# Sixteen of 22 input chunks of a down projection by seven products of sums of blocks

## The chip, the cores and the metric

The kernel runs on one core of a Trainium2 chip. Its time is device microseconds for one execution. The engines are TensorE (PE: matmuls; PEld: its weight loads), VectorE (DVE), ScalarE (ACT), GpSimd (POOL) and SyncE (SP, which here only starts DMAs). Each takes its own queue of instructions, and they wait for each other by semaphores. SBUF is the memory on the chip, PSUM the banks into which matmuls write (eight banks of 128 partitions x 512 float32).

## The reference

Two residual layers over 512 tokens of width 1024: the first mixes tokens by gated linear attention, the second by softmax attention. After each comes the same feed-forward block, in float32:

```python
def conv_ffn(h, w_up, w_conv, b_conv, w_down):
    u = h @ w_up                      # 1024 -> 2 x 2816
    u = depthwise conv of width 3 over tokens(u, w_conv) + b_conv
    val, gate = jnp.split(u, 2, axis=-1)
    return (jax.nn.silu(gate) * val) @ w_down      # 2816 -> 1024

x = x + conv_ffn(rmsnorm(x, norm_ffn[i]), ...)
```

2816 = 22 chunks of 128, and 1024 = 8 chunks of 128. The change is in the last product, `@ w_down`.

## The kernel before, in words

Data lie features by tokens: a tile has 128 features on the partitions and 512 tokens in the free dimension. The residual is held in eight tiles `x[0..7]`. A float32 product is made of three matmuls of a rounded type (float32r): each operand is split into a high part and a low part, and `mm3` (L266 to L268) adds high x high, high x low and low x high into one PSUM bank. Each matmul has a 128 x 128 weight block as its stationary operand and 512 tokens moving.

**Weights** come through the class `Weights`. A list `todo` holds them in the order of use. `make` loads 1 MB (16 blocks of 128 x 128) on SyncE's queue into one of two `raw` buffers (L118), and splits each half of it: the high part `wh` by ScalarE (L143), the low part `wl` by VectorE as raw minus high (L144), 128 x 1024 each, in three buffers of each. Some weights of the attention are split in another way: ScalarE writes the high part (L123) and the negative high part (L124), and an adding DMA started by GpSimd puts the raw weights on top (`flush`, L133). `half` returns the half that is wanted and makes one more ahead.

**The feed-forward block** `ffn` has two stages. In the first, for each m of 22, two `feature_tile`s (24 matmuls each) fill a bank with value and gate of chunk m (`up`). VectorE takes them out (`u`, L603), ScalarE and VectorE do the convolution (L605 to L607), ScalarE the silu (L609), VectorE the product (L610), and a split makes the high and low part (`gu`, L612 and L613) of chunk m. All 22 are kept in SBUF. In the second stage, for each output chunk c of 8, 22 `mm3` (one for each k) add up in one bank (`dn`); VectorE adds the bank to `x[c]` (L625), and the next stage's norm starts on that chunk (`nxt.chunk(c)`: scaled high part, low part, square), or, in the last layer, SyncE stores it.

The tile framework orders each engine's queue by priorities when the kernel is built, and puts in the semaphore waits. Banks come by name: `acc` three, `s` two, `pt` two, `po` one. `big` gives a 128 x 1024 tile from 22 buffers named `g`.

Of the kernel before, what the change touches and what calls it, by code (L numbers as in the profile page):

```python
# [8 lines left out]
F32 = mybir.dt.float32  # L9
# [26 lines left out]

O_STEPS = (22, 23, 25, 27, 29, 31, 32, 33, 34, 35, 36, 37)


# [7 lines left out]
def hybrid_encoder_kernel(  # L47
# [55 lines left out]
    class Weights:  # L103
# [6 lines left out]
        def add(self, src):  # L110
            for i in range(src.shape[0]):
                self.todo += [(src, i, 0), (src, i, 1)]

        def make(self, key):
            src, i, h = key
            if h == 0 and (id(src), i) not in self.raw:
                t = sp.tile([P, 4 * S], F32, tag="raw", bufs=2, name=nm("raw"))
                sync.dma_start(t, src[i])  # L118
                self.raw[id(src), i] = t
            r = self.raw[id(src), i][:, h * 2 * S : (h + 1) * 2 * S]  # L120
            hi, lo = pair("wh", 3, F32R, "wh"), pair("wl", 3, F32R, "wl")
            if any(src is a and i < n for a, n in self.by_dma):
                act.activation(hi, r, AF.Copy)  # L123
                act.activation(lo, r, AF.Copy, scale=-1.0)  # L124
# [20 lines left out]

        def half(self, src, n):
            key = (id(src), n // 2, n % 2)
            self.flush()
            while key not in self.made:
                self.make(self.todo.pop(0))  # L150
            if self.todo:
                self.make(self.todo.pop(0))
            return self.made.pop(key)

    W = Weights()
    up = [w_up[i] for i in range(2)]
    down = [w_down[i] for i in range(2)]
    for a in (w_vg, w_kq, w_gout, up[0], down[0]):
        W.add(a)
    qk_order = [w_akq[i : i + 1] for i in range(w_akq.shape[0])]  # L160
    for a in qk_order[:2] + [w_av] + qk_order[2:] + [w_aout, up[1], down[1]]:
        W.add(a)
    W.by_dma += [(a, 1) for a in qk_order + [w_av]] + [(w_aout, 2)]

# [114 lines left out]
    def feature_tile(*a):  # L279
        for _ in feature_steps(*a):  # L280
            pass
# [61 lines left out]
    def gla(norm, nxt):  # L343
# [40 lines left out]
        sync.dma_start(rraw, w_r)  # L384
        rw = pair("wh", 3, F32R, "rw")
        rv = rraw.rearrange("p (k o c) -> p k o c", k=KC, o=1)
# [199 lines left out]
    def ffn(layer, norm, cw, nxt):  # L586
        hl = []
        for m in range(FC):
            res, pss = [], []
            for t in range(2):  # L590
                ps = bank("s" if t else "acc", "up")
                feature_tile(*W.half(up[layer], 2 * m + t), norm.hl, ps)
# [17 lines left out]
            dve.tensor_tensor(res[0], res[0], res[1], ALU.mult)  # L610
            t = big(F32R, "gu")
            act.activation(t[:, :S], res[0], AF.Copy)  # L612
            dve.tensor_tensor(t[:, S:], res[0], t[:, :S].bitcast(F32), ALU.subtract)  # L613
            hl.append((t[:, :S], t[:, S:]))
        cur = None
        for c in range(KC):
            ps = bank("acc", "dn")
            for k in range(FC):
                u = c * FC + k
                if u % 8 == 0:  # L620
                    cur = W.half(down[layer], u // 8)
                sl = slice((u % 8) * P, (u % 8 + 1) * P)
                mm3(ps, cur[0][:, sl], cur[1][:, sl], *hl[k], k == 0, k == FC - 1)
            if nxt is not None or c < KC - 1:
                dve.tensor_tensor(x[c], x[c], ps, ALU.add)  # L625
                if nxt is not None:
                    nxt.chunk(c)
                else:
                    sync.dma_start(out[c * P : (c + 1) * P, :], x[c])
            else:  # L630
                for sl, queue in ((slice(0, S // 2), sync), (slice(S // 2, S), act)):
                    dve.tensor_tensor(x[c][:, sl], x[c][:, sl], ps[:, sl], ALU.add)
                    queue.dma_start(out[c * P : (c + 1) * P, sl], x[c][:, sl])


# [219 lines left out]
def _layout(inputs):  # L855
# [55 lines left out]
    dn = i["ffn_w_down"].reshape(2, FC, P, KC, P)  # L911
    dn = dn.transpose(0, 3, 1, 2, 4).reshape(2, KC * FC // 16, 16, P, P)
    a["w_down"] = con(dn.transpose(0, 1, 3, 2, 4).reshape(2, -1, P, 4 * S))
    return a
# [19 lines left out]
```

## Time and profile before

| what | value |
|---|---|
| median of 3 runs | 1133.23 us (1132.77 to 1133.43) |
| the profiled execution | 1133.16 us, its span 1131.4 us |
| TensorE busy | 1125.7 us (99%), 5260 matmuls |
| VectorE, ScalarE, GpSimd busy | 690.1, 482.1, 76.0 us |
| the two down projections | 528 matmuls each, the first matmuls at 469.5 and 1008.0 us of the span |
| granted TensorE clock | 1.0 |

A row of the profile names line, engine, operation, output <- inputs with shapes and a count; behind the bar are busy time in us, the mean ns of one, and the idle time of the engine just before such instructions, with what ended it. The chain names the work that ended last, followed back from the end. A timeline row has start and duration in us. The table by stretches has for each stretch its length, then each engine's busy us with the instruction count, the granted clock, the DMA share and GB/s.

### The profile page before, as it was taken

The numbers are of one execution on the slowest core, as the hardware profiler recorded it, in microseconds if no ns is written. First come the engines' busy times: TensorE is split into PE (matmuls) and PEld (weight loads), VectorE is DVE, ScalarE is ACT, GpSimd is POOL, SyncE is SP. The second block draws the span as 40 slices with busy tenths as digits, with TensorE's granted clock in tenths as the row PEclk, the third lists the DMA queues.
The fourth block names the chain that finished last, engine by engine and source line by source line (L and its number), as shares of the span: only waits on it lengthen the run. The fifth ranks groups of instructions, "written<-read, shape, count | busy, mean of one in ns | idle before, by whom it ended". The sixth has DMA issues, their size and how long they took to land.

```text
span 1131.4 us, 12991 instructions
## 1 busy us (share of the span) xinstructions
PE 1125.7 (99%) x5260; PEld 939.2 (83%) x5260; DVE 690.1 (61%) x996; ACT 482.1 (43%) x690; POOL 76.0 (7%) x66
## 2 busy tenths in 40 slices
PE   9999999999999999999999999999999999999998
PEld 7888888888888888888888888888888888888887
DVE  6787563677777777633325589766777777762221
ACT  5564232444444444422234667644444444442210
POOL 0104110000000000000004433000000000000000
PEclk9999999999999999999999999999999999999999
DMA  6422211232322323223247633223232232323320
GB/s 231 149 75 78 84 63 38 75 112 75 112 97 90 112 75 112 100 86 112 77 152 181 149 76 75 56 75 112 75 112 85 101 112 75 112 84 121 130 93 19
DMA packets 19980, 111.66 MB, mean 99 GB/s; under 512 B 2384, under 2 KB 3024, under 8 KB 8400
## 3 DMA queue, kind: packets, MB, share of 16 engines
q1 hardware_dynamic: 17328, 102.29, 25.9%
q0 software_dynamic: 2304, 8.39, 3.9%
q8 instruction: 41, 0.67, 0.2%
q10 hardware_dynamic: 288, 0.15, 0.0%
q14 instruction: 19, 0.16, 0.0%
HBM read 100.34 MB, written 2.10 MB: 91 GB/s over the span
## 4 chain that ended last, share of the span: by engine, by line
PE 99%; DVE 0%; DMA 0%; ACT 0%; issue 0%; SPq 0%; DVEq 0%; ACTq 0%
PE up L266 14%; PE up L267 14%; PE up L268 14%; PE vg L297 8%; PE op L323 8%; PE dn L266 7%; PE dn L268 7%; PE dn L267 7%; PE o L548 2%; PE pt L802 1%; PE av L297 1%; PE kv L524 1%; PE A L266 1%; PE A L268 1%; PE A L267 1%; PE B L266 1%
## 5 line engine op out<-in xcount | busy, mean ns | idle before, releaser
L143 ACT ACTIVATE wh<-raw 128x1024 fp32r<-128x1024 f32 x164 | 173.3, 1056 | 351.4 <-PE up L267 132.8
L144 DVE TENSOR_TENSOR wl<-raw,wh 128x1024 fp32r<-128x1024 f32 x164 | 203.7, 1242 | 144.8 <-ACT wh L143 144.6
L266 PE MATMUL up<-xhl,wh 128*128 128x512 f32 x704 | 274.3, 390 | 0.0
L268 PE MATMUL up<-xhl,wl 128*128 128x512 f32 x704 | 273.9, 389 | 0.0
L267 PE MATMUL up<-xhl,wh 128*128 128x512 f32 x704 | 273.9, 389 | 0.0
L268 PEld LDWEIGHTS up<-xhl,wl 128*128 128x128 f32 x704 | 132.2, 188 | 27.6
L266 PEld LDWEIGHTS up<-xhl,wh 128*128 128x128 f32 x704 | 132.2, 188 | 27.4
L267 PEld LDWEIGHTS up<-xhl,wh 128*128 128x128 f32 x704 | 132.2, 188 | 27.1
L266 PE MATMUL dn<-gu,wh 128*128 128x512 f32 x352 | 136.9, 389 | 0.0
L267 PE MATMUL dn<-gu,wh 128*128 128x512 f32 x352 | 136.9, 389 | 0.0
L268 PE MATMUL dn<-gu,wl 128*128 128x512 f32 x352 | 136.9, 389 | 0.0
L603 DVE TENSOR_TENSOR u<-up,R 128x512 f32<-128x512 f32 x88 | 60.3, 687 | 52.7 <-PE up L268 52.7
L297 PE MATMUL vg<-wh,xhl 128*128 128x512 f32 x256 | 79.7, 390 | 0.6 <-DVE halfneg L184 0.6
L605 ACT ACTIVATE y<-u,cw 128x512 f32<-128x512 f32 x88 | 71.2, 811 | 20.4 <-DVE u L603 20.4
L268 PEld LDWEIGHTS dn<-gu,wl 128*128 128x128 f32 x352 | 66.1, 188 | 13.8
L267 PEld LDWEIGHTS dn<-gu,wh 128*128 128x128 f32 x352 | 66.1, 188 | 13.7
L266 PEld LDWEIGHTS dn<-gu,wh 128*128 128x128 f32 x352 | 66.1, 188 | 13.6
L323 PE MATMUL op<-oT,wh 128*128 128x512 f32 x256 | 70.9, 395 | 0.0
L607 DVE SCALAR_TENSOR_TENSOR y<-u,cw,y 128x511 f32<-128x511 f32 x88 | 65.9, 751 | 2.9
L606 DVE SCALAR_TENSOR_TENSOR y<-u,cw,y 128x511 f32<-128x511 f32 x88 | 65.6, 746 | 0.6 <-ACT y L605 0.6
L609 ACT ACTIVATE y<-y 128x512 f32<-128x512 f32 x44 | 27.9, 634 | 87.8 <-DVE y L607 87.8
L297 PEld LDWEIGHTS vg<-wh,xhl 128*128 128x128 f32 x256 | 48.0, 188 | 10.6 <-ACT sq L240 0.7
(186 smaller groups left out, 1432.1 us busy)
## 6 DMA issues: line engine op xcount, KB each, us to landing
raw<-in_w_up_dram SPq DMA_DIRECT2D x44, 1024.0 KB, 4.8
raw<-in_w_down_dram SPq DMA_DIRECT2D x22, 1024.0 KB, 4.8
wl<-raw POOLq DMA_DIRECT2D x16, 512.0 KB, 4.7
raw<-in_w_vg_dram SPq DMA_DIRECT2D x6, 1024.0 KB, 4.7
raw<-in_w_akq_dram SPq DMA_DIRECT2D x5, 1024.0 KB, 5.2
raw<-in_w_kq_dram SPq DMA_DIRECT2D x4, 1024.0 KB, 4.8
raw<-in_w_gout_dram SPq DMA_DIRECT2D x4, 1024.0 KB, 4.8
raw<-in_w_aout_dram SPq DMA_DIRECT2D x4, 1024.0 KB, 4.9
```

The lines of the kernel that those rows point to most:

```text
L143: act.activation(hi[:, sl], r[:, sl], AF.Copy)
L144: dve.tensor_tensor(lo[:, sl], r[:, sl], hi[:, sl].bitcast(F32), ALU.subtract)
L266: mm(ps, wh, mh, start=start, stop=False)
L267: mm(ps, wh, ml, start=False, stop=False)
L268: mm(ps, wl, mh, start=False, stop=stop)
L297: mm(ps[j][:, :width], hl[k][i == 2][:, j * P : (j + 1) * P], (wl if i == 1 else wh)[:, sl], start=k == 0 and i == 0, stop=k == KC - 1 and ...
L323: mm(pss[ng][n], wt[:, sl], mv, start=k == 0 and i == 0, stop=k == KC - 1 and i == 2)
L603: dve.tensor_tensor(u, ps, norm.R, ALU.mult)
L605: act.activation(y, u, AF.Identity, scale=w(1), bias=w(3))
L606: dve.scalar_tensor_tensor(y[:, 1:], u[:, : S - 1], w(0), y[:, 1:], ALU.mult, ALU.add)
L607: dve.scalar_tensor_tensor(y[:, : S - 1], u[:, 1:], w(2), y[:, : S - 1], ALU.mult, ALU.add)
L609: act.activation(res[1], res[1], AF.Silu)
```

## The change: products of sums of blocks

The 2 x 2 blocks are: two input chunks (k = 2p, 2p+1), two output chunks (c = 2n, 2n+1), and two halves of the tokens (256 each). Before, such a block of the product takes eight half-width products. Now it takes seven, of sums and differences of blocks (Winograd's form of Strassen's scheme): four sums of weight blocks, four of token blocks, and the results are put together from running sums.

- Chunks 0 to 15 make eight pairs. `prepare` makes a pair's token-side sums (two on GpSimd, two on VectorE) and splits them: three `gu` tiles and half a tile for each pair.
- Pairs 0 to 3 are used in part 0, after the up chunk m = 9, and pairs 4 to 7 in part 1, after m = 17 (`DOWN_AFTER`). The pair of m = 8 and 9 is prepared inside part 0, after the second pair of outputs.
- A part has four output pairs n. For each, seven products of 4 chunk pairs x 3 matmuls, 256 tokens wide. Product 1 goes to bank r1; ScalarE copies r1 into r2, onto which product 6 adds; ScalarE copies r2 into the first half of r3, product 5 adds to r2, ScalarE copies r2 into the second half of r3, product 4 adds to r3's first half, product 3 to r2. Product 7 has its own bank r4, product 2 adds to r1. VectorE adds r1, r2, r3 and r4 into x[2n] and x[2n+1]. Product 1 of pair n+1 is issued ahead of product 3 of pair n.
- A 1 MB load of down weights now holds the 16 blocks of one n in one part. `summed` makes four pieces of it: piece 0 and 1 with VectorE sums and the split by ScalarE and VectorE, piece 2 (plain blocks) by ScalarE twice and the adding DMA of GpSimd, piece 3 half as wide. Up to three pieces are made ahead in a part, in four buffers of `wh` and of `wl` (three before). The scratch for GpSimd's DMA descriptors is set to 8192 bytes.
- Chunks 16 to 21 keep the `mm3` of 512 tokens, behind the last up chunk, in the order `PLAIN`: outputs 0 to 3 for k = 16 to 19, then k = 20 and 21 for these, then outputs 4 to 7.
- The host lays out the down weights in the new order.

```diff
+NQ, NPART = 4, 2
+PLAIN = ([(c, k) for c in range(4) for k in range(16, 20)] + [(c, k) for c in range(4) for k in (20, 21)]
+         + [(c, k) for c in range(4, 8) for k in range(16, 22)])
+DOWN_AFTER = {9: 0, 17: 1}
...
-            hi, lo = pair("wh", 3, F32R, "wh"), pair("wl", 3, F32R, "wl")
+            hi, lo = pair("wh", 4, F32R, "wh"), pair("wl", 4, F32R, "wl")
...
+        def summed(self, raw, sums, h):
+            a21, a11, a12, a22 = (raw[:, n * S : (n + 1) * S] for n in range(4))
+            if h == 0:
+                sums["e"] = e = big(F32, "sum")
+                dve.tensor_tensor(e[:, :S], a21, a22, ALU.add)
+                dve.tensor_tensor(a21, a21, a11, ALU.add)
+                r = raw[:, : 2 * S]
+            elif h == 1:
+                e = sums["e"]
+                dve.tensor_tensor(e[:, S:], e[:, :S], a11, ALU.add)
+                r = e
+            elif h == 2:
+                r = raw[:, 2 * S :]
+            else:
+                e = sums["e"]
+                r = tmp("sq", "sum4")
+                dve.tensor_tensor(r, e[:, S:], a12, ALU.add)
+                hi, lo = (sp.tile([P, S], F32R, tag="sq", bufs=3, name=nm(n)) for n in ("wh4", "wl4"))
+                act.activation(hi, r, AF.Copy)
+                dve.tensor_tensor(lo, r, hi.bitcast(F32), ALU.subtract)
+                return hi, lo
+            hi, lo = pair("wh", 4, F32R, "wh"), pair("wl", 4, F32R, "wl")
+            if h == 2:
+                act.activation(hi, r, AF.Copy)
+                act.activation(lo, r, AF.Copy, scale=-1.0)
+                self.pending.append((lo, r))
+            else:
+                act.activation(hi, r, AF.Copy)
+                dve.tensor_tensor(lo, r, hi.bitcast(F32), ALU.subtract)
+            return hi, lo
...
+        def prepare(p, y1, y2):
+            q = tmp("t", "q")
+            b11, b12, b21, b22 = y1[:, :H], y1[:, H:], y2[:, :H], y2[:, H:]
+            pool.tensor_tensor(q[:, :H], b22, b12, ALU.subtract)
+            pool.tensor_tensor(b12, b11, b12, ALU.subtract)
+            t = [big(F32R, "gu") for _ in range(3)]
+            if p % 2 == 0:
+                quads["half"] = big(F32R, "gu")
+            t4 = quads["half"]
+            split(y2, t[1])
+            split(y1, t[0])
+            dve.scalar_tensor_tensor(q[:, H:], b12, -1.0, b22, ALU.mult, ALU.subtract)
+            split(q, t[2])
+            dve.scalar_tensor_tensor(b21, q[:, H:], -1.0, b21, ALU.mult, ALU.subtract)
+            o = (p % 2) * H
+            split(b21, t4, o, H)
...
+        def down_part(part, then):
...
+            def product(n, i, dst, start):
+                h, o = PLACE[i]
+                if (n, h) not in pieces:
+                    pieces[n, h] = W.piece(src, part * NQ + n, h, 3)
+                wh, wl = pieces[n, h]
+                for j in range(NQ):
+                    sl = slice(o + j * P, o + (j + 1) * P)
+                    mh, ml = pairs[j][i]
+                    for a, (w, m) in enumerate(((wh, mh), (wh, ml), (wl, mh))):
+                        mm(dst, w[:, sl], m, start=start and j == 0 and a == 0, stop=j == NQ - 1 and a == 2,
+                           skip_group_check=True)
+                W.flush()
+            def begin(n):
+                r = st[n]
+                r[1] = bank("acc", "r1")
+                product(n, 1, r[1][:, :H], True)
+                r[2] = bank("acc", "r2")
+                act.activation(r[2][:, :H], r[1][:, :H], AF.Copy)
+            begin(0)
+            for n in range(NQ):
+                r, c, d = st[n], x[2 * n], x[2 * n + 1]
+                r1, r2 = r[1][:, :H], r[2][:, :H]
+                product(n, 6, r2, False)
+                r3 = bank("s", "r3")
+                act.activation(r3[:, :H], r2, AF.Copy)
+                r4 = bank("pt", "r4")
+                product(n, 7, r4[:, :H], True)
+                product(n, 2, r1, False)
+                product(n, 5, r2, False)
+                act.activation(r3[:, H:], r2, AF.Copy)
+                dve.tensor_tensor(c[:, :H], c[:, :H], r1, ALU.add)
+                product(n, 4, r3[:, :H], False)
+                if n + 1 < NQ:
+                    begin(n + 1)
+                two = lambda a: a.rearrange("p (o t) -> p o t", t=H)
+                dve.tensor_tensor(two(d), two(d), two(r4[:, :H]).to_broadcast([P, 2, H]), ALU.subtract)
+                dve.tensor_tensor(d, d, r3, ALU.subtract)
+                product(n, 3, r2, False)
+                dve.tensor_tensor(c[:, H:], c[:, H:], r2, ALU.add)
+                if n == 1 and then is not None:
+                    then()
...
+            if m in DOWN_AFTER:
+                down_part(DOWN_AFTER[m], (lambda: prepare(m // 2, last, y)) if m < 2 * NQ * NPART else None)
```

More of the change, by code (lines that the diff above doesn't have):

```diff
@@ L586, in ffn, with act_up @@
     def ffn(layer, norm, cw, nxt):
-        hl = []
-        for m in range(FC):
+        plain = {}
+        quads = {}
+        def act_up(m):
             res, pss = [], []
@@ L610, in ffn @@
             dve.tensor_tensor(res[0], res[0], res[1], ALU.mult)
[L611 to L623, printed above, removed]
+            return res[0]
@@ new lines, in ffn @@
+        PLACE = {1: (0, S), 7: (0, 0), 6: (1, S), 5: (1, 0), 2: (2, 0), 4: (2, S), 3: (3, 0)}
+        def down_part(part, then):
+            src = down[layer]
+            pairs = [quads.pop(part * NQ + i) for i in range(NQ)]
+            st = [{} for _ in range(NQ)]
+            pieces = {}
+            def product(n, i, dst, start):
[39 more added lines that the diff above has]
+                    then()
@@ L633, in ffn @@
                     queue.dma_start(out[c * P : (c + 1) * P, sl], x[c][:, sl])
+        last = None
+        for m in range(FC):
+            y = act_up(m)
+            if m >= 2 * NQ * NPART:
+                t = big(F32R, "gu")
+                split(y, t)
+                plain[m] = (t[:, :S], t[:, S:])
+            elif m % 2 == 0:
+                last = y
+            elif m not in DOWN_AFTER:
+                prepare(m // 2, last, y)
+            if m in DOWN_AFTER:
+                down_part(DOWN_AFTER[m], (lambda: prepare(m // 2, last, y)) if m < 2 * NQ * NPART else None)
+        cur, open_ = None, {}
+        for u, (c, k) in enumerate(PLAIN):
+            if u % 8 == 0:
+                cur = W.half(down[layer], NPART * NQ * 2 + u // 8)
+            sl = slice((u % 8) * P, (u % 8 + 1) * P)
+            if c not in open_:
+                open_[c] = bank("s" if c == 3 else "acc", "dn")
+            mm3(open_[c], cur[0][:, sl], cur[1][:, sl], *plain[k], k == 2 * NQ * NPART, k == FC - 1)
+            if k == FC - 1:
+                end(c, open_[c])
     def attention(norm, nxt):
```

64 lines of the change are left out of this document (50 added, 14 removed).

## The prediction

> **What bounds the kernel now.** I read the page's busy shares first, then the chain that ended last, then the groups of the down projection.
>
> ```profile
> PE 1125.7 (99%) x5260; PEld 939.2 (83%) x5260; DVE 690.1 (61%) x996; ACT 482.1 (43%) x690; POOL 76.0 (7%) x66
> ...
> PE 99%; DVE 0%; DMA 0%; ACT 0%; issue 0%; SPq 0%; DVEq 0%; ACTq 0%
> PE up L266 14%; PE up L267 14%; PE up L268 14%; PE vg L297 8%; PE op L323 8%; PE dn L266 7%; PE dn L268 7%; PE dn L267 7%; PE o L548 2%; PE pt L802 1%; PE av L297 1%; PE kv L524 1%; PE A L266 1%; PE A L268 1%; PE A L267 1%; PE B L266 1%
> ...
> L266 PE MATMUL dn<-gu,wh 128*128 128x512 f32 x352 | 136.9, 389 | 0.0
> L267 PE MATMUL dn<-gu,wh 128*128 128x512 f32 x352 | 136.9, 389 | 0.0
> L268 PE MATMUL dn<-gu,wl 128*128 128x512 f32 x352 | 136.9, 389 | 0.0
> ```
>
> TensorE is the whole chain, and the down projection never waits (idle 0.0). So a matmul taken away is worth its full step, and a wait put into TensorE's queue costs its full length. The 389 ns is the latency of one matmul, not its step: matmuls overlap. The step comes from the table by stretches, and that of a half-width matmul from the only long run of them, the attention's values (av).
>
> ```profile
> core 0: us, PE busy (x) PEld busy (x) DVE busy (x) ACT busy (x) POOL busy (x), PEclk, DMA share, GB/s
> ...
> 600.00:770.00 170.00, 169.74 (x967) 145.06 (x966) 121.59 (x247) 101.92 (x175) 42.45 (x34) 1.00 0.39 101
> ...
> 613.90:625.30 11.40, 11.40 (x96) 11.37 (x95) 8.46 (x11) 6.91 (x10) 4.89 (x4) 1.00 0.53 144
> 250.00:450.00 200.00, 200.00 (x884) 165.62 (x883) 145.05 (x186) 88.63 (x111) 0.00 (x0) 1.00 0.29 100
> ```
>
> ```profile
> 614.09 11.52 PE av L297 x96
> ```
>
> ```profile
> L297 PE MATMUL av<-wh,xhl 128*128 128x256 f32 x64 | 11.7, 283 | 0.0
> ```
>
> Width 512 steps 200.00/884 = 0.226 us. Width 256 steps 11.52/96 = 0.120 us by the chain, not 0.113: halving the width saves 47%, because each matmul carries about 0.013 us that does not shrink. The granted clock is 1.00 in both stretches.
>
> **The saving on TensorE.** Per layer 16 chunks x 8 outputs x 3 matmuls = 384 of width 512 go: 384 x 0.2262 = 86.9 us. In come 2 parts x 4 output pairs x 7 products x 4 chunk pairs x 3 = 672 of width 256: 672 x 0.1200 = 80.6 us. That leaves 6.2 us a layer, 12.4 us in both. One product is 12 matmuls, 1.44 us; an output pair is 7 products, 10.1 us.
>
> [...]
>
> **What hides beside TensorE.** Prices:
>
> ```profile
> 350.06 0.69 DVE L603 TENSOR_TENSOR u<-up,R 128x512 f32<-128x512 f32 x1 [1.31 <-PE up L268]
> ...
> 354.37 0.69 DVE L610 TENSOR_TENSOR y<-y,y 128x512 f32<-128x512 f32 x1 [0.76 <-ACT y L609]
> 355.76 0.69 DVE L613 TENSOR_TENSOR gu<-y,gu 128x512 fp32r<-128x512 f32 x1 [0.70 <-ACT gu L612]
> 356.37 0.68 DVE L603 TENSOR_TENSOR u<-up,R 128x512 f32<-128x512 f32 x1
> 356.97 1.22 DVE L144 TENSOR_TENSOR wl<-raw,wh 128x1024 fp32r<-128x1024 f32 x1
> 358.10 0.75 DVE L606 SCALAR_TENSOR_TENSOR y<-u,cw,y 128x511 f32<-128x511 f32 x1
> 358.88 0.75 DVE L607 SCALAR_TENSOR_TENSOR y<-u,cw,y 128x511 f32<-128x511 f32 x1
> ```
>
> ```profile
> L143 ACT ACTIVATE wh<-raw 128x1024 fp32r<-128x1024 f32 x164 | 173.3, 1056 | 351.4 <-PE up L267 132.8 <-PE dn L267 127.5 <-PE op L323 34.0
> L605 ACT ACTIVATE y<-u,cw 128x512 f32<-128x512 f32 x88 | 71.2, 811 | 20.4 <-DVE u L603 20.4
> L609 ACT ACTIVATE y<-y 128x512 f32<-128x512 f32 x44 | 27.9, 634 | 87.8 <-DVE y L607 87.8
> ...
> L525 ACT ACTIVATE sa<-kv 128x256 f32<-128x256 f32 x8 | 3.1, 384 | 8.3 <-PE kv L524 8.3
> ```
>
> ```profile
> L441 DVE TENSOR_TENSOR ga<-ga,t 128x256 f32<-128x256 f32 x8 | 3.3, 418 | 0.0
> ```
>
> ```profile
> L482 POOL TENSOR_TENSOR end<-ek,fk 128x384 f32<-128x384 f32 x8 | 8.4, 1066 | 4.8 <-DVE ek L478 4.8
> ```
>
> Back to back on VectorE a 512-wide operation takes 0.60 (356.37 to 356.97), a 1024-wide one 1.13, a scalar-tensor-tensor 0.78. In the up projection a pair of chunks adds 0.60 + 0.42 + 2 x 0.42 = 1.9 us of VectorE to 2 x 10.9 us. VectorE was busy 145 of 200 us, so it goes from 73% to 81%; two GpSimd operations of about 1066 x 256/384 = 711 ns a pair lie beside it. TensorE there needs only the weight pieces, which the fourth buffer lets run further ahead: I charge nothing, and if that cover went, 8 pairs x 1.9 x 2 = 30 us bounds it. In a part, an output pair costs VectorE 4 x 0.60 (sums) + 2 x 1.13 + 0.60 (low parts) + 2 x 0.42 + 2 x 0.60 (into x), 7.3 us, and ScalarE 4 x 1.06 + 0.63 + 3 x 0.38 = 6.0 us: both fit 10.1 us, but not by much, so order in the queues decides. The remaining plain stage keeps the 0.226 us step; its last chunk is wanted 17 x 3 x 0.226 = 11.5 us after the last up matmul and is ready 6.4 us after it (350.06 to 356.45): free.
>
> **What the new waits cost.** TensorE now waits for ScalarE's copies between banks, and ScalarE and VectorE take their queues in order. I followed the built order of each engine. Three places:
>
> (a) *Start of a part.* Product 6 adds onto r2, which ScalarE first copies from r1. In ScalarE's queue that copy stands behind the activation for the second half of the last up chunk (m = 9 or 17), and that one waits for VectorE. Count from the end of up's first half for m = 8 (TensorE 0; the part starts at 3 x 5.43 = 16.3). VectorE is late from preparing pair 3: its chain runs 5.0 us to the product y (350.06 to 355.06), then two GpSimd operations, ScalarE copies and five VectorE operations, 8.9 us in all from 5.4 us earlier, so 3.5. Then 21 operations stand before the activation's input: 13 x 0.60 + 6 x 0.78 + 2 x 1.13 = 14.7, so 18.2; activation 0.81 and copy 0.38 give 19.4. TensorE is there at 16.3 + (12 + 5) x 0.12 = 18.3, five matmuls of r4 being put between. Stall 1.1 us; in part 1 the copies of the third weight piece and of the fourth's high part stand in ScalarE's queue in its place, and the same count gives 19.4 against 18.3 again. Bounds: 0 if VectorE is on time, 2.4 with the full durations (0.69, 0.75, 1.22) in place of the steps, 1.3 more. Four parts: 4.4 us.
>
> (b) *r3 before product 4.* Product 5 ends r2, ScalarE copies it into r3, product 4 needs r3. In the built order the high part of the next pair's third weight piece goes first, and its buffer is freed by that same product 5: 0.16 (a result lands 0.283 - 0.120 after the next start) + 1.06 + 0.38 + 0.05 to pass on = 1.65 against the 11 matmuls of the next product 1, 1.32: 0.33, and a restart.
>
> ```profile
> 701.18 0.50 PE L266 MATMUL s<-k,q 128*128 128x512 f32 x1 [0.26 <-ACT p L784]
> 701.51 0.39 PE L267 MATMUL s<-k,q 128*128 128x512 f32 x1
> ```
>
> The restart is 0.33 between starts instead of 0.23, 0.1. So 0.4 a time, three times in part 0; in part 1 the first has no cover, 0.16 + 0.38 + 0.1 = 0.65, then twice 0.4. The fourth pair has three up matmuls as cover in both. Sum 2.65 a layer, 5.3 us. Bounds: 0, if r3's copy were first, and 1.0 each (16 us) if nothing covered.
>
> (c) *The low part by DMA.* The third piece gets its low part as ScalarE's negative copy plus an adding DMA.
>
> ```profile
> 623.13 1.04 ACT L124 ACTIVATE wl<-raw 128x1024 fp32r<-128x1024 f32 x1
> ```
>
> ```profile
> 624.47 0.87 POOL L133 DMA_DIRECT2D wl<-raw  x1 [2.86 <-ACT wl L124]
> ```
>
> ```profile
> wl<-raw POOLq DMA_DIRECT2D x16, 512.0 KB, 4.7
> ```
>
> ```profile
> DMA to landing us min/median/max: 4.5/4.7/9.1
> ```
>
> From product 5's end: 0.16 + 1.06 + 0.38 + 1.05 + 0.3 (624.17 to 624.47) + 4.7 = 7.65. Its first reader comes 62 matmuls later, 7.44, plus the 0.4 of (b): 7.84. So 0.2 us of slack; in part 1's second pair, where VectorE also waits for a load behind this DMA, it is late by about 0.2: 0.4 us in two layers.
>
> Sum: 4.4 + 5.3 + 0.4 = 10.1 lost of 12.4 gained, **2.3 us faster**. The profiled execution was 1133.16 us (span 1131.4, 1.8 around it), 0.07 under the median of 1133.23, so 1130.8.
>
> **The rivals.**
>
> *The waits are hidden.* If VectorE starts each part on time (a) goes, and (b) shrinks to the copies: 1133.2 - 12.4 + 0 to 6 = 1121 to 1127, middle 1124. For it: TensorE lost 0.26 us in the whole attention stage (600 to 770), with VectorE 72% and ScalarE 60% busy.
>
> *The adding DMA decides (slower).* Every pair but a part's first takes its low part from a DMA with 0.2 us to spare; 12 pairs do. A landing of 4.9 us is the point from which it costs; against it, the median is 4.7 and no load need run beside it, since the next load waits for this very DMA. For it: the longest landing was 9.1. At 6.0, 1.1 x 12 = 13 us more: 1144.
>
> *VectorE is later at the start of a part (slower, small).* GpSimd beside VectorE and the full durations make (a) 2.4 to 3.5 instead of 1.1: 5 to 10 us more, 1136 to 1140.
>
> *The step halves.* In a long run 256 might cost 0.2262/2 = 0.113: 672 x 0.007 = 4.7 us a layer, 1121.4. [...] The 96 matmuls of av are long enough that I give it little.
>
> **How the numbers follow.** This kernel's measurement can tell about 0.2%, 2.3 us, from no change. Forecast case (1127 to 1135): 0.42; waits hidden: 0.24; adding DMA: 0.14; VectorE later: 0.18; halved step 0.02. Faster by over 0.2% (under 1130.9): 0.21 + 0.24 + 0.02 = 0.47. Slower (over 1135.5): 0.14 + 0.18, with 0.01 of the forecast's upper tail, 0.33. The same: 0.20. Range 1122 to 1142: it cuts the far end of the hidden case and of the DMA case.
>
> **What would show it.** Steps of r1 to r4 matmuls at 0.120; idle of TensorE in front of r2 of about 1 us released by ScalarE once a part (a), in front of r3 0.3 to 0.6 us three times a part (b), and next to none released by DMA at r1 (c). Without idle at r2 the first rival holds; with idle at r1 after a DMA the second. A step off 0.120 by 0.007 moves the result by 9 us, and idle in the up projection would mean that VectorE's 81% was not free.

## The result, and the profile after

The changed kernel takes 1136.93 us (median of 6 runs, 1136.25 to 1139.34), the kernel before 1133.15 us beside it (6 runs, 1132.77 to 1135.96). The ratio is 1.0032, 95% interval 1.0019 to 1.0045: 3.8 us slower. The profiled execution took 1136.9 us with a span of 1135.2 us, at a granted clock of 1.00.

The page of the kernel after: busy shares, the chain by engine, and the adding DMAs.

```profile
PE 1119.9 (99%) x5836; PEld 957.2 (84%) x5836; DVE 793.1 (70%) x1204; ACT 551.2 (49%) x818; POOL 121.4 (11%) x114
...
PE 86%; DVE 6%; DMA 2%; issue 2%; ACT 2%; POOL 1%; SPq 0%; DVEq 0%; ACTq 0%; POOLq 0%
...
wl<-raw POOLq DMA_DIRECT2D x32, 512.0 KB, 4.6
```

TensorE is still 99% busy, but the chain has changed: before, it was TensorE for 99%, now for 86%. VectorE, ScalarE, GpSimd and DMAs have come into it. A chain that leaves the fullest engine runs through the places where that engine waits. Where they lie is told by the starts of the stages on TensorE. Timeline of the kernel after: the first matmul of feed-forward 0, of the attention, of feed-forward 1, and the last matmul.

```profile
230.47 0.39 PE L332 MATMUL up<-xhl,wh 128*128 128x512 f32 x1
...
591.91 0.39 PE L332 MATMUL A<-xhl,wh 128*128 128x512 f32 x1
...
769.87 0.39 PE L332 MATMUL up<-xhl,wh 128*128 128x512 f32 x1
...
1130.88 0.39 PE L334 MATMUL dn<-gu,wl 128*128 128x512 f32 x1
```

The same four rows of the kernel before.

```profile
228.76 0.39 PE L266 MATMUL up<-xhl,wh 128*128 128x512 f32 x1
...
589.22 0.39 PE L266 MATMUL A<-xhl,wh 128*128 128x512 f32 x1
...
767.17 0.39 PE L266 MATMUL up<-xhl,wh 128*128 128x512 f32 x1
...
1127.40 0.39 PE L268 MATMUL dn<-gu,wl 128*128 128x512 f32 x1
```

| stage on TensorE | before, us | after, us | difference |
|---|---|---|---|
| up to the first up matmul | 228.76 | 230.47 | +1.71 |
| feed-forward 0 | 360.46 | 361.44 | +0.98 |
| attention | 177.95 | 177.96 | 0.0 |
| feed-forward 1 | 360.23 | 361.01 | +0.78 |
| behind the last matmul, to the end of the span | 4.0 | 4.3 | +0.3 |

So each feed-forward block, which was to gain 6.2 us, lost almost 1. And the stage ahead of it, which the diff doesn't seem to touch, lost 1.7.

The granted clock and the step of the new products, in two stretches of the kernel after (columns as before: length, busy us and count of each engine, clock, DMA share, GB/s).

```profile
252.00:340.00 88.00, 88.00 (x389) 72.85 (x389) 70.33 (x102) 43.42 (x58) 7.91 (x9) 1.00 0.24 84
372.00:380.60 8.60, 8.60 (x74) 8.60 (x73) 5.09 (x7) 3.98 (x6) 0.86 (x1) 1.00 0.55 137
```

In the second, TensorE steps through 256-wide products without a wait; from start to start nearly all of them are 0.12 us apart. The first lies in the up projection: TensorE never idles there, with VectorE at 80%. The saving was there, and waits took more than all of it. The waits by line, kernel after (total us, times, longest):

```profile
PE r L730 <- ACT r L739: 5.7, 4, 1.6
...
PE z L483 <- DVE rst L472: 1.3, 1, 1.3
PE r L730 <- ACT r L752: 1.0, 2, 0.5
PE r L730 <- DVE wl L174: 0.9, 2, 0.6
...
PE r L730 <- DMA wl<-raw: 0.2, 1, 0.2
```

This view counts only idle time. What a wait costs is seen in the starts: the part's length, less 336 steps of 0.12 and three up matmuls of 0.226 put into it, leaves 2.49 and 4.85 us lost in parts 0 and 1 of layer 0, 2.69 and 4.43 in layer 1; 14.5 in all. Each wait in it carries another 0.10 us of restart.

**The first copy of a part.** Timeline of the kernel after, start of part 0 on TensorE, VectorE and ScalarE:

```profile
342.00 0.28 PE L730 MATMUL r<-gu,wl 128*128 128x256 f32 x1
...
344.13 0.50 PE L730 MATMUL r<-gu,wh 128*128 128x256 f32 x2 [1.25 <-ACT r L739]
...
342.27 0.69 DVE L672 TENSOR_TENSOR u<-up,R 128x512 f32<-128x512 f32 x1
...
342.99 0.81 ACT L674 ACTIVATE y<-u,cw 128x512 f32<-128x512 f32 x1 [1.27 <-DVE u L672]
343.71 0.36 ACT L739 ACTIVATE r<-r 128x256 f32<-128x256 f32 x1
```

The copy of r1 into r2 (L739) needs none of these up values: r1's last matmul (342.00) was done at 342.3, 1.4 us earlier. It waits because it is queued behind the activation, and that waits for VectorE. In the starts the wait is 1.41 us in part 0 and 1.78 in part 1, and 0.10 more each for the restart.

**The ring behind the adding DMA.** A stretch of the chain of the kernel after, part 1 of layer 0:

```profile
472.43 4.56 DMA wl<-raw
...
477.12 4.99 DMA raw<-in_w_down_dram
...
482.82 1.79 DVE wl L174 x2
484.61 4.93 DMA wl<-raw
...
489.59 3.85 PE r L730 x30
```

The adding DMA reads `raw`, so the next load into that buffer starts only when it has landed (476.98). VectorE's sum for the pair after next waits for that load, and the low parts of the next pair are queued behind this sum. TensorE's first reader of the next adding DMA starts 0.05 us after it has landed. From 472.43 to 489.59 no TensorE work is in the chain. The chain puts that second DMA behind VectorE; the timeline of VectorE and ScalarE has more:

```profile
482.13 0.69 DVE L150 TENSOR_TENSOR sum<-raw 128x512 f32<-128x512 f32 x1 [1.15 <-DMA raw<-in_w_down_dram]
...
482.33 1.05 ACT L169 ACTIVATE wh<-raw 128x1024 fp32r<-128x1024 f32 x1
483.27 1.04 ACT L170 ACTIVATE wl<-raw 128x1024 fp32r<-128x1024 f32 x1
```

The DMA (484.61) follows ScalarE's negative copy, which ended at 484.31; 15 of the 16 adding DMAs of the parts start about 0.3 us behind that copy. So VectorE's wait of 1.15 us makes low parts late, and it is ScalarE's queue that makes this DMA late.

**The stage ahead.** Timeline of the kernel before, around the gate weights (`gst`) of the first mixer:

```profile
32.48 0.21 DVE L379 CAST smask<-gconst 128x128 uint8<-128x128 f32 x1
...
30.22 2.39 POOL L395 TENSOR_TENSOR gst<-graw,gst 32x1024 fp32r<-32x1024 f32 x1
...
28.57 1.04 ACT L394 ACTIVATE gst<-graw 128x1024 fp32r<-128x1024 f32 x1
```

And of the kernel after:

```profile
32.56 2.36 DVE L445 CAST smask<-gconst 128x128 uint8<-128x128 f32 x1
...
32.43 2.40 POOL L461 TENSOR_TENSOR gst<-graw,gst 32x1024 fp32r<-32x1024 f32 x1 [2.22 <-ACT gst L460]
...
30.28 1.06 ACT L190 ACTIVATE wh<-raw 128x1024 fp32r<-128x1024 f32 x1 [6.11 <-DMA raw<-in_w_vg_dram]
31.25 1.04 ACT L460 ACTIVATE gst<-graw 128x1024 fp32r<-128x1024 f32 x1
...
39.37 0.47 PE L483 MATMUL z<-rst,gst 128*128 128x512 f32 x1 [1.31 <-DVE rst L472]
```

With a fourth buffer, ScalarE's split of one more weight half may stand ahead of the gate weights, and it waits until 30.28 for its load. The copy of the gate weights follows it 2.7 us later than before, and GpSimd's subtraction 2.2 us later. That now falls beside VectorE's small cast, which took 0.21 us and now takes 2.36. Everything behind it on VectorE is late, and `z`, which had no wait, waits 1.31 us.

### The profile page after: what moved, and what is told of

Same layout as the page of the kernel before. It is cut to its first block, busy times and chain, and to the rows that moved or that the text cites. A ratio compares the mean times of both kernels' runs of the same rounds, so it can differ in the third digit from the quotient of the medians.

```text
span 1135.2 us, 14636 instructions
## 1 busy us (share of the span) xinstructions
PE 1119.9 (99%) x5836; PEld 957.2 (84%) x5836; DVE 793.1 (70%) x1204; ACT 551.2 (49%) x818; POOL 121.4 (11%) x114
## 4 chain that ended last, share of the span: by engine, by line
PE 86%; DVE 6%; DMA 2%; issue 2%; ACT 2%; POOL 1%; SPq 0%; DVEq 0%; ACTq 0%; POOLq 0%
PE r L730 12%; PE up L333 12%; PE up L332 12%; PE up L334 11%; PE op L389 8%; PE vg L363 7%; PE dn L334 2%; PE dn L333 2%; PE dn L332 2%; PE o L614 2%; DMA wl<-raw 1%; PE pt L968 1%; PE av L363 1%; PE kv L590 1%; DMA raw<-in_w_down_dram 1%
## 5 line engine op out<-in xcount | busy, mean ns | idle before, releaser
L190 ACT ACTIVATE wh<-raw 128x1024 fp32r<-128x1024 f32 x132 | 139.0, 1056 | 212.7 <-PE up L333 114.3
L191 DVE TENSOR_TENSOR wl<-raw,wh 128x1024 fp32r<-128x1024 f32 x132 | 163.8, 1241 | 52.4 <-ACT wh L190 52.4
L730 PE MATMUL r<-gu,wh 128*128 128x256 f32 x896 | 164.5, 285 | 7.1 <-ACT r L739 5.7
L730 PEld LDWEIGHTS r<-gu,wh 128*128 128x128 f32 x896 | 139.1, 191 | 11.8 <-ACT r L739 6.6
L730 PE MATMUL r<-gu,wl 128*128 128x256 f32 x448 | 125.5, 285 | 1.1 <-DVE wl L174 0.9
L730 PEld LDWEIGHTS r<-gu,wl 128*128 128x128 f32 x448 | 84.9, 191 | 2.3 <-DVE wl L174 1.3
L180 POOL DMA_DIRECT2D wl<-raw x32 | 28.2, 881 | 303.6 <-ACT wl L138 140.4
L389 PEld LDWEIGHTS op<-oT,wh 128*128 128x128 f32 x256 | 47.1, 188 | 9.7 <-ACT oT L629 0.3
```

The lines of the kernel that those rows point to most:

```text
L190: act.activation(hi[:, sl], r[:, sl], AF.Copy)
L191: dve.tensor_tensor(lo[:, sl], r[:, sl], hi[:, sl].bitcast(F32), ALU.subtract)
L389: mm(pss[ng][n], wt[:, sl], mv, start=k == 0 and i == 0, stop=k == KC - 1 and i == 2)
L730: mm(dst, w[:, sl], m, start=start and j == 0 and a == 0, stop=j == NQ - 1 and a == 2, skip_group_check=True)
```

## The experiments

"Lost in parts" is worked out as above, from the starts, for parts 0 and 1 of layer 0 and of layer 1. Medians of the kernel before, in the same batches, were 1133.3 to 1133.7 us.

**1. The small cast behind the critical operations.** Only the order of one VectorE operation differs from the kernel after.

```diff
-        dve.tensor_copy(smask, tri)
...
+        ready = dve.tensor_tensor(rst[32:64, :], rf[32:64, :], rst[32:64, :].bitcast(F32), ALU.subtract)
+        with tc.issue_after(ready.ins):
+            dve.tensor_copy(smask, tri)
```

> The changed kernel with one instruction moved: VectorE's cast of the triangular mask (0.21 us before, 2.36 us after the change, beside GpSimd's 2.4 us subtraction) is queued behind the operation on which the first gate matmul z waits. Theory (1.7 us of the loss lies ahead of the feed-forward blocks, in this cast): TensorE's 1.31 us idle in front of z goes, the first up matmul starts at 228.8 us again instead of 230.5, and the whole is 1.5 to 1.8 us faster than the changed kernel, about 1135.3. Rival (the fourth weight buffer delays the gate chain in ScalarE's queue too, by the split of a weight half put ahead of the gate weights): z still waits, for ScalarE or GpSimd, and at most 0.5 us comes back.

1137.58 us (1136.78 to 1139.41), ratio 1.0043 (1.0026 to 1.0060). Timeline of this kernel:

```profile
33.31 3.09 DVE L191 TENSOR_TENSOR wl<-raw,wh 128x1024 fp32r<-128x1024 f32 x1
...
32.92 2.40 POOL L460 TENSOR_TENSOR gst<-graw,gst 32x1024 fp32r<-32x1024 f32 x1 [1.97 <-ACT gst L459]
...
39.72 0.47 PE L484 MATMUL z<-rst,gst 128*128 128x512 f32 x1 [0.91 <-DVE rst L471]
```

My theory, that the cast itself was dear, fell. The operation that came into its place, 1.22 us elsewhere, took 3.09. It ended at 36.4, GpSimd's subtraction at 35.3: as if its own 1.2 us had begun only then. So it is the place beside GpSimd's subtraction that costs, not the cast.

**2. The buffers alone.** The kernel before with four `wh` and `wl` buffers and the 8192-byte scratch, nothing else.

```diff
-            hi, lo = pair("wh", 3, F32R, "wh"), pair("wl", 3, F32R, "wl")
+            hi, lo = pair("wh", 4, F32R, "wh"), pair("wl", 4, F32R, "wl")
...
```

> The kernel before with the fourth buffer of high and low weight parts and the smaller descriptor scratch alone, no sums of blocks. Theory: the reordering at the start comes from the fourth buffer, so the first up matmul starts 1.7 us later and the whole is 1.5 to 1.8 us slower than before, about 1134.8, with the feed-forward blocks unchanged. Rival (the start is slower for something that comes with the sums, such as the order in which weights are asked for): the time of before within 0.5 us.

1134.51 us (1134.03 to 1134.78), ratio 1.0010 (1.0000 to 1.0019). Timeline:

```profile
32.30 2.13 DVE L379 CAST smask<-gconst 128x128 uint8<-128x128 f32 x1
...
38.88 0.47 PE L417 MATMUL z<-rst,gst 128*128 128x512 f32 x1 [1.07 <-DVE rst L406]
```

The same wait, without any of the new products, and both feed-forward blocks unchanged (360.46 and 360.23 us). The first up matmul starts at 229.85, 1.1 us late. So 1.1 of the 1.7 us lost ahead of the feed-forward blocks come with the buffers (and the scratch, which this run does not separate from them).

**3. The first copy ahead.** The epilogue of the last up chunk (VectorE and ScalarE) is queued behind the copy.

```diff
-            begin(0)
+            copy = begin(0)
+            with tc.issue_after(copy.ins):
+                late()      # the epilogue of the last up chunk
```

> The changed kernel with ScalarE's first copy r1 to r2 of each part queued ahead of the convolution and activation of the up chunk that was just finished (these are issued behind it). Theory (ScalarE's order costs TensorE 1.4 us in part 0 and 1.8 us in part 1 plus a restart each time, 6.7 us in four parts): these four waits fall under 0.3 us each and the whole is 4.5 to 6.5 us faster than the changed kernel, 1130.4 to 1132.4. Rival (ScalarE and VectorE have too much to do at the start of a part, whatever the order): the wait comes back in front of r3, or for the low parts by VectorE, and less than 2 us is won.

1137.12 us (1136.75 to 1137.59), ratio 1.0034 (1.0021 to 1.0047). Lost in parts: 1.52, 5.88, 1.40, 5.77. In part 0 the first wait fell from 1.41 to 0.14, as the theory has it. In part 1 it fell to 0.79, and what it had hidden came out. The waits of this kernel that end with a DMA, by line, and one of them in the timeline:

```profile
PE r L733 <- DMA wl<-raw: 3.8, 4, 1.0
```

```profile
476.15 0.39 PE L733 MATMUL r<-gu,wl 128*128 128x256 f32 x1 [0.88 <-DMA wl<-raw]
```

TensorE was early and met the adding DMA (0.2 us by this view before). The rival, that the wait moves, was right in part 1, though the wait went to the DMA, which it had not named; the sum stayed.

**4. r3's copy ahead of the next third piece.** Product 4 goes behind the next pair's product 1, and the weight pieces behind the copy.

```diff
-                act.activation(r3[:, H:], r2, AF.Copy)
+                whole = act.activation(r3[:, H:], r2, AF.Copy)
...
-                product(n, 4, r3[:, :H], False)
                 if n + 1 < NQ:
-                    begin(n + 1)
+                    with tc.issue_after(whole.ins):
+                        begin(n + 1)
+                product(n, 4, r3[:, :H], False)
```

> The changed kernel with two orders set in each part: the copy into the second half of r3 goes ahead of the high part of the next pair's third weight piece on ScalarE, and product 4 is issued behind the whole of the next pair's product 1. Theory (that order costs 0.3 us three times in part 0 and 0.78 + 0.3 + 0.3 us in part 1): waits in front of r3 go, 3 to 4.5 us faster than the changed kernel, 1132.4 to 1134. Rival (the adding DMA has no slack): its landing is later by the 0.4 us of the copy and more, TensorE waits for DMA in front of r1 once a pair, and less than 1.5 us is won.

1137.47 us (1136.16 to 1138.72), ratio 1.0037 (1.0024 to 1.0050). Lost: 2.31, 4.07, 2.79, 5.41. The waits at r3 in part 0 are gone (the first one of part 1 stays), and waits for the DMA of 0.43, 0.97, 0.44 and 0.84 us have come. Again the rival: in all twelve turns from one pair to the next, TensorE's first reader of the low part now loads its weights 0.04 to 0.05 us after the landing, so the ring has no slack to give.

**5. Products 5 and 2 exchanged.** Product 5 is the last reader of the buffer into which the next third piece is made, and product 2 the first reader of that piece.

```diff
-                product(n, 2, r1, False)
                 product(n, 5, r2, False)
                 act.activation(r3[:, H:], r2, AF.Copy)
+                product(n, 2, r1, False)
```

> The changed kernel with products 2 and 5 of each output pair exchanged: product 5 (and ScalarE's copy into the second half of r3) goes ahead of product 2. Theory A (a ring sets the pace: product 5 of one pair frees the buffer of the next pair's third weight piece, then 0.16 + 1.06 + 0.38 + 1.05 + 0.3 + 4.7 = 7.7 us of copies and adding DMA, then products 2 and 5 of the next pair, 2.9 us, 10.5 us round against 10.1 us of matmuls; so in the earlier runs a wait that was taken away in front of r3 came back in front of r1): with product 2 behind product 5 the ring is 7.7 + 1.4 us and no longer holds, product 2 covers the copy into r3, the parts lose 1.5 us each (the first copy) plus the low-part wait of part 1 instead of 2.5 and 4.6, and the whole is 4 to 6.5 us faster than the changed kernel, 1130.5 to 1133. Rival B (VectorE is what is late in the parts): waits for the low parts by VectorE take their place, less than 2 us is won.

1132.99 us (1131.52 to 1134.66), ratio 0.9997 (0.9987 to 1.0006): 4 us less than the kernel after. Lost: 2.13, 2.63, 2.14, 3.50. The waits of its new products in the view by line:

```profile
PE r L730 <- ACT r L739: 5.8, 4, 1.7
...
PE r L730 <- ACT r L747: 0.3, 1, 0.3
```

The rows for the DMA, for VectorE's low part and for product 5's copy have gone from it (in the starts product 5's copy still costs 0.24 us once in each part 0, and a DMA under 0.1 us once in each part 1); the four first copies have stayed about as they were. By the starts, with restarts, the waits for DMAs and low parts fell from 2.3 to 0.3 us and those at r3 from 4.5 to 1.6, and about 1 us of new waits came in front of product 5. Moving one line has given the DMA room, but the larger part of the gain is that product 2 now covers the copy into r3.

**6. The third piece's low part by VectorE.** No adding DMA in the parts.

```diff
-            if h == 2:
-                act.activation(hi, r, AF.Copy)
-                act.activation(lo, r, AF.Copy, scale=-1.0)
-                self.pending.append((lo, r))
-            else:
-                act.activation(hi, r, AF.Copy)
-                dve.tensor_tensor(lo, r, hi.bitcast(F32), ALU.subtract)
+            act.activation(hi, r, AF.Copy)
+            dve.tensor_tensor(lo, r, hi.bitcast(F32), ALU.subtract)
```

> The changed kernel with the low part of the third weight piece made by VectorE (raw minus high, 1.13 us) instead of ScalarE's negative copy and the adding DMA. Theory A (the ring through the DMA sets the pace): the ring shrinks to 0.2 + 1.06 + 1.24 + 2.9 us and cannot hold, the next load no longer waits for the DMA's landing; waits in front of r1 go and part 1 loses about 1.5 us less, the whole 2 to 4 us faster than the changed kernel, 1133 to 1135. Rival B (VectorE is what is late): 1.13 us more of it an output pair costs up to 4 us a part, 1138 or more.

1131.86 us (1131.65 to 1132.55), ratio 0.9985 (0.9976 to 0.9995): 5 us less than after. Lost: 1.52, 3.51, 1.53, 3.50. The waits for the DMA are gone with it. Most of the gain lies elsewhere: ScalarE has an operation fewer too, and the first copy waits only 0.33 and 0.14 us, 5.5 us less in the four parts with the restarts. Against that, in part 1 the second half of r3 waits 1.84 us, since ScalarE's queue holds operations there that wait for VectorE.

**7. The gate weights first.** Only the start of the first mixer: ScalarE's copy of the gate weights is queued ahead of the weight halves.

```diff
-        act.activation(gst, graw[:, : 2 * S], AF.Copy)
+        gate_hi = act.activation(gst, graw[:, : 2 * S], AF.Copy)
...
-        seg_out(seg(1, beside), v, 1)
+        with tc.issue_after(gate_hi.ins):
+            ps = seg(1, beside)
+        seg_out(ps, v, 1)
```

> The changed kernel with one order set at the start: ScalarE's copy that makes the gate weights' high part goes ahead of the weight halves that are asked for after it. Theory (the fourth buffer let a weight half, waiting for its load until 30.3 us, stand ahead of it; so GpSimd's subtraction of 2.4 us came 2.2 us later, beside a VectorE operation that then took as long as GpSimd, whichever it was, and the gate chain was late): GpSimd's subtraction runs by 28 to 31 us, no VectorE operation beside it takes over 1.3 us, z waits under 0.2 us, 1.1 to 1.5 us faster than the changed kernel, about 1135.5. Rival (two-input VectorE operations and GpSimd always hold each other up): the wait moves to the operation that now stands beside it and nothing is won.

1136.42 us (1135.39 to 1139.19), ratio 1.0024 (1.0013 to 1.0035). The trace shows what was wanted: `z` does not wait, the cast takes 0.22 us, the first up matmul starts at 229.12, 1.35 us earlier than in the kernel after. The median is only 0.5 us lower, less than the runs scatter. In the profiled execution one adding DMA of layer 1 landed 6.7 us after its issue and cost TensorE 1.73 us, which hides the gain. Whether the full 1.35 us reach the end can't be read from this run alone. That the start itself is earlier shows in the other traces: in the six kernels with this edit (7 to 12) the first up matmul starts at 228.68 to 229.45, in the five with the order of the kernel after (that kernel and 3 to 6) at 229.68 to 230.55.

**8. Three edits together**: 3, 5 and 7.

> Three edits together on the changed kernel: products 2 and 5 exchanged, the first copy r1 to r2 of a part ahead of the last up chunk's convolution, and the gate weights' high part ahead of the next weight half on ScalarE. Theory A: part 0 loses under 0.6 us, part 1 under 3, and the start 0.3 instead of 1.5 us: 1125 to 1129, under the kernel before. Rival B (VectorE late at the start of a part): part 1 keeps 4 us or more, 1130 to 1133.

1128.01 us (1127.89 to 1128.51), ratio 0.9948 (0.9934 to 0.9963). Lost: 0.60, 2.89, 0.59, 2.97. Edit 3 alone had gained nothing, edit 5 four us; on top of 5, the parts lose 3.4 us less than with 5 alone. What is left, by line:

```profile
PE r L735 <- ACT r L744: 1.3, 2, 0.6
PE r L735 <- DVE wl L174: 1.0, 2, 0.5
PE r L735 <- DMA wl<-raw: 0.7, 2, 0.4
```

**9. Four edits**: 3, 5, 6 and 7.

> The kernel of e7 (products 2 and 5 exchanged, first copy of a part first, gate weights first) with the low part of the third piece by VectorE as well. Theory A (ScalarE's order and the ring through the adding DMA cost the time, VectorE has room): part 1's waits for DMA (0.5 us) and for the first copy (0.8 us, ScalarE has one operation of 1.04 us fewer in front) go too, 1126 to 1127.5. Rival B (VectorE is next): 1.13 us more an output pair brings waits for low parts, 1128 to 1130.

1133.39 us (1132.87 to 1135.46), ratio 1.0000 (0.9992 to 1.0009): 5 us more than with three. Lost: 2.46, 3.29, 2.36, 4.34. My theory fell; the rival was right in direction, but too small, and most of the waits are at first copies, not at the low parts that it named. Timeline of the start of part 1:

```profile
470.27 1.22 DVE L169 TENSOR_TENSOR wl<-raw,wh 128x1024 fp32r<-128x1024 f32 x1
471.41 0.69 DVE L162 TENSOR_TENSOR sum<-sum,raw 128x512 f32<-128x512 f32 x1
...
472.13 0.63 ACT L164 ACTIVATE wh<-sum 128x512 fp32r<-128x512 f32 x1 [2.27 <-DVE sum L162]
472.66 0.36 ACT L739 ACTIVATE r<-r 128x256 f32<-128x256 f32 x1
...
473.08 0.50 PE L730 MATMUL r<-gu,wh 128*128 128x256 f32 x2 [1.54 <-ACT r L739]
```

VectorE's added low part (470.27) puts off the sum of the fourth piece, ScalarE's high part of it waits 2.27 us, and the first copy stands behind that. The order that helped with the DMA hurts without it.

**10. The same without the first copy ahead**: 5, 6 and 7.

> The same without the first copy of a part put ahead (exchanged products, low part by VectorE, gate weights first). Theory A: with the negative copy gone from ScalarE's queue the first copy is late by 0.1 to 0.4 us a part only, as in the run with the low part by VectorE alone, so within 1.5 us of e9. Rival (the queue behind the last up chunk is what makes it late): 1.2 us or more a part, 4 us over e9.

1131.21 us (1130.57 to 1133.31), ratio 0.9981 (0.9972 to 0.9990). Lost: 1.79, 2.95, 1.81, 3.57. It is 2.2 us faster than 9, which neither expectation had. The wait at the first copy is down to 0.33 and 0.14, but 1.23 and 0.74 us appear at the next copies (ScalarE, L744 and L748). The edits don't add up; that all of them order the same two queues would explain it.

**11. The fourth piece behind the first copy**, on top of the three edits.

```diff
-                product(n, 1, r[1][:, :H], True)
+                product(n, 1, r[1][:, :H], True, 3 if n else 2)   # pieces made ahead
```

> The version with products 5 and 2 exchanged, the first copy ahead and the gate weights first, in which also the first pair's fourth weight piece is made behind the first copy of a part. Theory A (an order on ScalarE holds the first copy): in part 1 the 0.63 us high part of the fourth piece, which waits for VectorE's sum, no longer stands ahead of the first copy, so the 0.79 us wait falls to 0.1 to 0.2 as in part 0; 2 x 0.6 to 0.7 = 1.3 us less, 1126 to 1127.5, beside 1128 of the version without this. Rival B (the wait moves): the fourth piece's sum comes later on VectorE, so the raw buffer comes free later and the waits at the second pair (VectorE's low part 0.68, the DMA 0.52) grow by as much or more: 1128 to 1130.

1128.15 us (1127.65 to 1130.01), ratio 0.9957 (0.9945 to 0.9970). Lost: 0.59, 2.87, 0.59, 3.10, and 0.8 at the first copy of part 1 as before. The edit did not do what it says: ScalarE's queue came out with the fourth piece's high part still ahead of the copy, every instruction where it was. So this run tells nothing of that wait.

**12. The three edits a second time.**

> The version with products 5 and 2 exchanged, the first copy ahead and the gate weights first, a second time. Theory A: 1127.5 to 1129, about 5 us under the kernel before, and the same waits as in its first run (0.6 us lost in part 0, 2.9 in part 1). If its first run was a favourable draw: 1130 to 1133.

1128.57 us (1128.05 to 1130.18), ratio 0.9961 (0.9947 to 0.9974), lost 0.60, 2.88, 0.60, 3.33. Experiment 11 ran the same order, so the version of the three edits, in three measurements, is 4.7 to 5.4 us faster than the kernel before.

## Why the prediction was right or wrong

It forecast 2.3 us faster, at 1130.8, and the kernel came out 3.8 us slower, at 1136.93, inside the range but on the other side. Three steps failed: term (a) was too small by 2.4 us, term (c) by 1.9, and the start of the kernel, which lost 1.7, had no term. Point by point:

- *The saving* was right. The step of a 256-wide matmul is 0.120 us in the parts too, so the arithmetic gave its 12.4 us. The halved step did not occur. The Trainium skill (TensorE: Matmul & The Clock Gate, "Back-to-back issue gap") gives N/2.4 + 2.5 ns as the gap of an isolated matmul and sets it apart from a sustained stream. For 256 columns that is an estimate of 109 ns by this page, and the stream here stepped 120.
- *Nothing charged in the up projection* was right: no idle TensorE there, with VectorE at 80% (forecast 81%).
- *(a), the start of a part*, had the right mechanism and too small a size: 4.4 us forecast, 6.8 measured (1.41 and 1.78, each with 0.10 of restart, in two layers). In part 0 the activation began 0.4 us after the count and I had left out the restart that I priced in (b). In part 1 two activations and the fourth piece's high part between them stood ahead of the copy, where I had counted the one activation's place. Experiment 3 shows the mechanism: with the copy ahead of these, the wait falls to 0.14 in part 0 and 0.79 in part 1. (The bound of 2.4 adds 1.3 us for the full durations; its own figures give 13 x 0.09 + 2 x 0.09 - 6 x 0.03 = 1.2.)
- *(b), r3 before product 4*, was about right: 5.3 forecast, 4.5 measured (0.15 to 0.20 a time, and 0.68 for the first of part 1, which was counted as 0.65 with its restart; each has 0.10 of restart on top). Timeline of ScalarE in the kernel after, with the order that was read from the build:

```profile
359.86 1.06 ACT L169 ACTIVATE wh<-raw 128x1024 fp32r<-128x1024 f32 x1 [1.88 <-PE r L730]
360.82 0.36 ACT L752 ACTIVATE r<-r 128x256 f32<-128x256 f32 x1
```

- *(c), the low part by DMA*, forecast 0.4 us in all; measured some 2.3 us (0.72 and 0.50 for VectorE's low part, 0.32 and 0.14 for the DMA in part 1, 0.15 once in part 0, each with its restart). "So 0.2 us of slack" was near the mark: of the twelve turns from one pair to the next, the DMA landed 0.2 to 0.5 us ahead of its reader in seven, was late by under 0.1 in two and by 0.14 to 0.32 in three. What was mis-sized is the second pair of part 1, put at 0.2 us a layer: it cost 1.2 and 0.8. There VectorE waits 1.15 us for the load that the first DMA holds back through `raw`, with the pair's low parts queued behind that wait. And the third piece's high part, which the count put ahead of the copy into r3, began 2.3 us behind the start of that copy (480.02, 482.33), with pieces 0 and 1 ahead of it on ScalarE.
- *The ring as a whole*. I followed one DMA from product 5 to its first reader, and not on to the next product 5. Product 5 frees the buffer of the next pair's third piece, the copies and the DMA follow (7.65 us in the forecast), then products 2 and 5 of that pair (2.9 us): a ring of 10.5 us for each pair, against 10.1 of the pair's own matmuls. In the kernel after it measured about 10.0 (medians: 7.2 from the third piece's high part to the landing, 2.8 from the first reader to the next high part), beside turns of 10.4 that include the waits at r3. So it does not set the pace of every turn there, but it leaves almost no room: experiments 3 and 4 took other waits away and met it. How much of the 2.3 us belongs to the ring and how much to the two late queues is not separated, since experiments 5 and 6 also changed the waits at r3 and at the first copy.
- Small waits of under 0.1 us and their restarts add 0.9. So 14.5 lost in place of 10.1.
- *Outside the block* there was no term at all, and there the prediction lost another 1.7 us. "Up to three pieces are made ahead, in four buffers" was read as a change of the down projection. But the four buffers serve every weight of the kernel, and the order of ScalarE's queue in the first mixer changed with them. Experiment 2 shows 1.1 us of it by itself, and 7, where the old order brings the first up matmul forward by 1.35, that the order is the cause.

6.1 us between forecast and result are thus 4.4 of waits in the parts, 1.7 in the first mixer and 0.3 behind the last matmul, less 0.3 by which these sums miss the measured stages. The rival whose time came nearest, VectorE later at the start of a part (1136 to 1140), asked for (a) of 2.4 to 3.5 us; it was 1.5 to 1.9 and would have given 1133 alone. It was not that rival either, but three terms together. VectorE's lateness has a share in (c), though: in part 0 the third piece of the first pair was begun 3.6 us before the part, in part 1 only 0.4 us (470.14, the part at 470.56), shortly after ScalarE had waited 1.41 us for one of VectorE's sums. How large that share is was not measured.

The adding DMA decides, the slower rival, did not hold: its median landing was 4.6 us, not 6, and the waits that end with a DMA cost 0.9 us with their restarts.

What stays open: the last 2.9 us in part 1 of the best version were not taken away, since the edit of experiment 11 moved nothing. And in experiments 9 and 10 only the wait at the first copy of part 1 in experiment 9 was followed to its cause.

## What to carry to other kernels

When a change makes the fullest engine wait for others, follow each buffer round the whole ring (last reader, copy, DMA, next load, first reader) and hold its length against the work of one turn; if it is as long, taking a wait away elsewhere may only uncover the ring, as in experiments 3 and 4. Copies on which TensorE waits belong ahead of epilogues in an in-order queue, but judge that order again whenever work moves from one engine to another. A pool that gets one more buffer can change the order of other stages that draw from it, as in the first mixer here: look at those too.

## What the runs showed of the hardware

After each wait of over 0.1 us in the parts of the kernel after, the first step of 256-wide matmuls took 0.22 us in place of 0.12.

A VectorE operation on SBUF that began beside GpSimd's subtraction (32 x 1024) ended a little less than its own length after that subtraction: the cast, 0.21 us elsewhere, took 2.36 and ended 0.09 us after it, and the low part, 1.22 elsewhere, took 3.09 and ended 1.08 after it, while GpSimd's own 2.39 to 2.40 stayed. In the kernel before, the same subtraction began at 30.22, beside four scalings out of PSUM on VectorE, and nothing was lost. The kernel before, timeline of VectorE, and the kernel after, where GpSimd's subtraction came only at 32.43:

```profile
29.84 2.72 DVE L366 TENSOR_SCALAR v<-vg,rtok 128x512 f32<-128x512 f32 x4
```

```profile
29.91 2.73 DVE L432 TENSOR_SCALAR v<-vg,rtok 128x512 f32<-128x512 f32 x4
```

The Trainium skill (SBUF — State Buffer, "Who interferes with whom") has a rule for this: GpSimd shares a port pair with VectorE. A VectorE instruction with two SBUF inputs contends with a GpSimd instruction that reads SBUF, and so does a copy or cast in a two-port mode; the one that starts first has the pair for its whole length. A VectorE instruction with at most one SBUF input outside those modes does not contend. The low part with its two SBUF inputs and the scalings out of PSUM agree with this here. The cast agrees if it ran in such a mode, which no run shows.
